# Argmax, gather and scatter: staging space first, spread list lanes, and row copies and zero scatters on semaphores of their own

## The chip, the cores and the metric

The kernel runs on one core of a Trainium2 chip. The metric is the time of the program on the device in microseconds. The span that the profile prints is about 2 us shorter than the time of the run.

## The reference

```python
def setup_inputs():
    B, S, H = (8, 2048, 2560)
    return {'scores': randn(B, S, S), 'values': randn(B, S, H)}     # float32

def reference(scores, values):
    best_j = np.argmax(scores, axis=2)
    b_idx = np.arange(B)[:, None]
    gathered = values[b_idx, best_j, :].copy()
    out = np.zeros_like(values)
    np.add.at(out, (b_idx, best_j, slice(None)), gathered)
    return out
```

Row j of a batch's output is its row of `values` times the number of score rows whose maximum lies at j. So the kernel counts the winners, and then each output row of 10,240 bytes is one of three things: count 0, a row of zeros; count 1, a copy of the row; count 2 or more, the row times the count.

## The kernel before

Counting: a tile of scores (256 rows, 2 MB, so 64 tiles in all and eight to a batch) comes in on the SP queue. DVE finds the maximum of each row and its place, and four small matmuls at a time add one-hot products into `cnt`. There are ten places for a tile: seven buffers of a pool, and three in `vbig`, the staging space that the values will use later. Before, loads 7, 8 and 9 go into `vbig`:

```python
    def count_steps(b, cnt_ps):
        for u in range(NT // R):                      # 8 tiles of a batch
            x = b * NT // R + u - NB                  # NB = 7, NX = 3
            if 0 <= x < NX:
                s_tile = vbig[:, x * R * S:(x + 1) * R * S]
            else:
                s_tile = spool.tile([P, R * S], FP32, name="s_tile")[:]
            nc.sync.dma_start(out=s_tile, in_=scores[...])
            ...                                       # max, max_index; a yield after each row
```

Values: when a batch is counted, its rows are sorted into lists. Rows of count 0 get a rank, and so do those of count 2 or more; rank r stands on lane (partition) r mod 128 in column r div 128. A transfer that POOL issues takes one column of 128 indices; an index outside of the bounds is skipped: its row doesn't move. Rows of count 1 need no rank: their 16 transfers copy straight from DRAM to DRAM.

```python
    def value_steps(b, cnt_ps):
        ...
        one_i = fin.tile([P, NT], INT32)              # a pool of two buffers
        ...
        for t in range(4):
            copy_once(t)
        ...                                           # ranks
        oh = ohp.tile([P, 2 * NT, P], FP16)
        nc.vector.tensor_tensor(out=oh[:], in0=lo[:]...,      # lo = rank & 127
            in1=lane_f[:].unsqueeze(1)..., op=ALU.is_equal)   # lane_f[lane] = lane
        ...
        for k in range(MCAP):                         # 5 columns of count >= 2
            v = stage()                               # one sixth of vbig
            gather(v, mi[:, k:k + 1])
            nc.scalar.activation(out=v, in_=v, ..., scale=mc[:, k:k + 1])
            staged.append(v)
            copy_once(next(rest))
        for k in range(ZCAP):                         # 7 columns of count 0
            scatter(zrow[:], zi[:, k:k + 1])
            copy_once(next(rest))
        for k in range(MCAP):
            scatter(staged[k], mi[:, k:k + 1])
        yield

        # ---- main loop
        for b in range(B):
            cnt_ps = psum_c.tile([P, NT], FP32)
            for _ in count_steps(b, cnt_ps):
                next(pending, None)                   # the values of b-1, between rows of b
            for _ in pending:
                pass
            pending = value_steps(b, cnt_ps)
```

The framework derives all waits from this program order: whoever comes later in it and touches the same memory waits for whoever comes earlier. Every transfer that POOL issues takes one of eight semaphores in turn, so POOL waits until the transfer issued eight before has landed.

## Time and profile before

| | before |
|---|---|
| time, median | 889.1 us |
| moved by the DMA engines | 347.05 MB, mean 391 GB/s |
| busy: DVE / POOL / ACT / PE | 687 / 290 / 103 / 18 us |
| DVE's longest single wait | 19.0 us, for `one_i` |

A DMA row of the slices is the mean of sixteen engines. A share of 0.95 can mean sixteen engines that are nearly always busy, or fifteen that wait for one.

### The profile page before, as it was taken

To read this page: it belongs to the slowest core of one execution; us is meant where nothing else is said; L and a number is where in the kernel's file an instruction comes from. 1 tells how busy PE (TensorE), PEld (TensorE's weight loads), DVE (VectorE), ACT (ScalarE), POOL (GpSimd) and SP (SyncE) were. 2 spreads that over 40 slices of the span, in tenths; PEclk is the share of its full clock that TensorE was granted. 3 is DMA by queue.
4 is the path that set the end of the run, shared out by engine and by line. 5 is a ranking of instruction groups with operands and counts; after the bars stand their busy time and mean duration, and the time that the engine had idled before them with its cause. 6 is when DMAs were issued, how large, how long until landed. Compare 5 with 4: busy or idle time off the path is not lost.

```text
span 888.3 us, 2271 instructions
## 1 busy us (share of the span) xinstructions
PE 18.0 (2%) x400; PEld 17.0 (2%) x400; DVE 687.3 (77%) x740; ACT 103.4 (12%) x43; POOL 290.3 (33%) x271
## 2 busy tenths in 40 slices
PE   0000000000000000000000000000000000000000
PEld 0000000000000000000000000000000000000000
DVE  6999999999999999999749994899919999000000
ACT  2000032000121000031001310023000500400500
POOL 0000452232323221521254222542234545544540
DMA  9998379999999999999999999999999998999994
GB/s 378 433 430 364 122 315 409 428 423 425 427 424 412 397 412 373 342 411 427 396 391 378 423 431 420 407 418 426 427 407 366 407 396 345 393 423 408 423 403 185
DMA packets 47248, 347.05 MB, mean 391 GB/s; under 512 B 18278, under 2 KB 18278, under 8 KB 18278
## 3 DMA queue, kind: packets, MB, share of 16 engines
q0 software_dynamic: 38016, 212.67, 59.2%
q1 hardware_dynamic: 9216, 134.22, 36.1%
q14 instruction: 13, 0.11, 0.0%
q8 instruction: 3, 0.05, 0.0%
HBM read 354.42 MB, written 293.60 MB: 729 GB/s over the span
## 4 chain that ended last, share of the span: by engine, by line
DMA 62%; DVE 28%; issue 4%; POOL 2%; POOLq 0%; DVEq 0%
DMA out_dram<-zrow,zero_i 31%; DMA vbig<-in_values_dram,many_i 12%; DVE am L147 12%; DMA out_dram<-vbig,many_i 12%; DVE mx L146 11%; DMA out_dram<-in_values_dram,one_i 6%; DVE oh L215 2%; POOL out_dram L33 1%; DMA s_tile<-in_scores_dram 1%; DVE oh_lo L156 1%; POOL vbig L113 1%; POOL out_dram L118 1%; DVE lo L152 0%; DVE rz L223 0%; DVE oh_hi L160 0%
## 5 line engine op out<-in xcount | busy, mean ns | idle before, releaser
L146 DVE MAX8 mx<-s_tile 128x8 f32<-128x2048 f32 x122 | 278.1, 2279 | 6.5 <-DMA s_tile<-in_scores_dram 6.5
L147 DVE FIND_INDEX8 am<-mx,s_tile 128x8 uint32<-128x2048 f32 x122 | 278.8, 2285 | 0.0
L33 POOL DMA_INDIRECT out_dram<-in_values_dram,one_i x128 | 129.2, 1009 | 249.3 <-DMA out_dram<-in_values_dram,one_i 103.3
L255 ACT ACTIVATE vbig<-vbig,many_c 128x2560 f32<-128x2560 f32 x40 | 97.1, 2428 | 737.6 <-DMA vbig<-in_values_dram,many_i 737.5
L118 POOL DMA_INDIRECT out_dram<-zrow,zero_i x56 | 57.9, 1034 | 159.4 <-DMA out_dram<-zrow,zero_i 77.4
L113 POOL DMA_INDIRECT vbig<-in_values_dram,many_i x40 | 60.0, 1501 | 82.2 <-DMA out_dram<-vbig,many_i 36.9
L118 POOL DMA_INDIRECT out_dram<-vbig,many_i x40 | 42.6, 1064 | 85.0 <-DMA out_dram<-zrow,zero_i 61.7
L179 DVE CAST one_i<-one_f 128x16 int32<-128x16 f32 x8 | 1.6, 196 | 52.8 <-DMA out_dram<-in_values_dram,one_i 52.2
L215 DVE TENSOR_TENSOR oh<-lo,lane_f 128x4096 f16<-128x4096 uint32 x8 | 35.4, 4426 | 0.0
L156 DVE TENSOR_TENSOR oh_lo<-lo,lane_f 128x512 bf16<-128x512 uint32 x32 | 22.2, 694 | 0.3
L165 PE MATMUL cnt_ps<-oh_hi,oh_lo 128*128 128x16 bf16 x128 | 8.1, 174 | 558.3 <-DVE oh_hi L160 558.3
L165 PEld LDWEIGHTS <-oh_lo 128*128 128x128 bf16 x128 | 8.4, 105 | 558.0 <-DVE oh_lo L156 556.9
L147 DVE MATCH_VALUE_LOAD am<-mx,s_tile 128x8 f32 x122 | 11.2, 92 | 4.2
L147 DVE FIND_INDEX8 am<-mx,vbig 128x8 uint32<-128x2048 f32 x6 | 13.7, 2285 | 0.0
L146 DVE MAX8 mx<-vbig 128x8 f32<-128x2048 f32 x6 | 13.7, 2281 | 0.0
L160 DVE TENSOR_TENSOR oh_hi<-hi,lane_f 128x64 bf16<-128x64 uint32 x32 | 7.0, 219 | 0.0
L234 PE MATMUL m_ps<-rm,oh 128*128 128x16 f16 x128 | 4.8, 175 | 86.0 <-DVE rm L230 86.0
L152 DVE TENSOR_SCALAR lo<-am 128x4 uint32<-128x4 uint32 x32 | 5.6, 176 | 1.1
L234 PEld LDWEIGHTS <-oh 128*128 128x128 f16 x128 | 4.1, 105 | 86.6 <-DVE rm L230 75.3
L154 DVE TENSOR_SCALAR hi<-am 128x4 uint32<-128x4 uint32 x32 | 5.6, 174 | 0.0
L237 PE MATMUL z_ps<-rz,oh 128*128 128x16 f16 x128 | 4.6, 174 | 0.0
L237 PEld LDWEIGHTS <-oh 128*128 128x128 f16 x128 | 4.0, 104 | 0.0
(50 smaller groups left out, 55.7 us busy)
## 6 DMA issues: line engine op xcount, KB each, us to landing
s_tile<-in_scores_dram SPq DMA_DIRECT2D x61, 2048.0 KB, 12.0
vbig<-in_scores_dram SPq DMA_DIRECT2D x3, 2048.0 KB, 38.9
out_dram<-in_values_dram,one_i POOLq DMA_INDIRECT x128
out_dram<-zrow,zero_i POOLq DMA_INDIRECT x56
vbig<-in_values_dram,many_i POOLq DMA_INDIRECT x40
out_dram<-vbig,many_i POOLq DMA_INDIRECT x40
```

What stands on the lines that cost most here:

```text
L33: return eng.add_instruction(ins)
L113: nc.gpsimd.indirect_dma_start(out=v, out_offset=None, in_=values_flat[:, :], in_offset=bass.IndirectOffsetOnAxis(ap=idx, axis=0), bounds_ ...
L118: writes_out(nc.gpsimd.indirect_dma_start(out=out_flat[:, :], out_offset=bass.IndirectOffsetOnAxis(ap=idx, axis=0), in_=v, in_offset=None, ...
L146: nc.vector.max(out=mx[:], in_=rows)
L147: nc.vector.max_index(out=am[:, g, :], in_max=mx[:], in_values=rows)
L156: nc.vector.tensor_tensor(out=oh_lo[:], in0=lo[:].unsqueeze(2).to_broadcast([P, G, P]), in1=lane_f[:].unsqueeze(1).to_broadcast([P, G, P]) ...
L160: nc.vector.tensor_tensor(out=oh_hi[:], in0=hi[:].unsqueeze(2).to_broadcast([P, G, NT]), in1=lane_f[:, 0:NT].unsqueeze(1).to_broadcast([P, ...
L165: nc.tensor.matmul(out=cnt_ps[:], lhsT=oh_lo[:, g, :], rhs=oh_hi[:, g, :], start=(t == 0), stop=(t == NT - 1))
L215: nc.vector.tensor_tensor(out=oh[:], in0=lo[:].unsqueeze(2).to_broadcast([P, 2 * NT, P]), in1=lane_f[:].unsqueeze(1).to_broadcast([P, 2 * ...
L234: nc.tensor.matmul(out=m_ps[:], lhsT=oh[:, NT + t, :], rhs=rm[:, t, :, :].rearrange("p a k -> p (a k)"), start=(t == 0), stop=(t == NT - 1))
L237: nc.tensor.matmul(out=z_ps[:], lhsT=oh[:, t, :], rhs=rz[:, t, :], start=(t == 0), stop=(t == NT - 1))
L255: nc.scalar.activation(out=v, in_=v, func=mybir.ActivationFunctionType.Copy, bias=0.0, scale=mc[:, k:k + 1])
```

## The change

Its intent, in three parts. First, scores use the staging space at once, for loads 0 to 2, and a second time for loads 10 to 12; batch 0's values are made in one block, before batch 1 is counted, with all 16 copies first, then zeros, then gathers. Second, the ranks of a column are spread over the lanes by a table `fill_f`, so that a column that is not full has work on all sixteen DMA engines. Third, copies and zero scatters get one semaphore per batch, outside the limit of 8 in flight, and POOL waits for all of them once at the end. The core of the diff (cuts marked):

```diff
+    for a in range(4):
+        first, step = (a >> 1) + 8 * (a & 1) + 16 * (a & 1), 16 - 32 * (a & 1)
+        nc.gpsimd.iota(fill_i[:, a * 32:(a + 1) * 32].rearrange("p (x y z) -> p x y z", x=4, y=2),
+                       pattern=[[2, 4], [step, 2], [32, 4]], base=first, channel_multiplier=0)
...
+    def free_running(b):
+        def note(ins):
+            writes_out(ins)
+            ins.then_inc(landed[b], 16)
+            tc.info.no_tile_sem_insts.add(ins.ins.name)
+            n_free[b] += 1
+        return note
...
-            x = b * NT // R + u - NB
-            if 0 <= x < NX:
+            x = b * NT // R + u
+            if x < 2 * (NX + NB) and x % (NX + NB) < NX:
+                x %= NX + NB
...
-        one_i = fin.tile([P, NT], INT32)
+        one_i = ones_i[:, b * NT:(b + 1) * NT]
...
-            writes_out(scatter_rows_in_dram(
+            free_running(b)(scatter_rows_in_dram(
...
-        for t in range(4):
+        first = NT if b == 0 else 4
+        for t in range(first):
             copy_once(t)
...
-            in1=lane_f[:].unsqueeze(1).to_broadcast([P, 2 * NT, P]), op=ALU.is_equal)
+            in1=fill_f[:].unsqueeze(1).to_broadcast([P, 2 * NT, P]), op=ALU.is_equal)
...
+        for part in (zeros, gathers) if b == 0 else (gathers, zeros):
+            part()
...
             pending = value_steps(b, cnt_ps)
+            if b == 0:
+                for _ in pending:
+                    pass
...
+    for b in range(B):
+        nc.gpsimd.wait_ge(landed[b], 16 * n_free[b])
```

More of the change, by code (lines that the diff above doesn't have):

```diff
@@ L75 @@
     nc.gpsimd.iota(lane_i[:], pattern=[[1, P]], base=0, channel_multiplier=0)
+    fill_i = consts.tile([P, P], INT32)
+    for a in range(4):
+        first, step = (a >> 1) + 8 * (a & 1) + 16 * (a & 1), 16 - 32 * (a & 1)
+        nc.gpsimd.iota(fill_i[:, a * 32:(a + 1) * 32].rearrange("p (x y z) -> p x y z", x=4, y=2),
+                       pattern=[[2, 4], [step, 2], [32, 4]], base=first, channel_multiplier=0)
     part_i = consts.tile([P, 1], INT32)
@@ L83 @@
     nc.vector.tensor_copy(lane_f[:], lane_i[:])
+    fill_f = consts.tile([P, P], FP32)
+    nc.vector.tensor_copy(fill_f[:], fill_i[:])
     part_f = consts.tile([P, 1], FP32)
@@ L95 @@
     nc.vector.memset(zero1[:], 0.0)
-    zrow = consts.tile([P, H], FP32)
+    zrow = ctx.enter_context(nc.sbuf_tensor([P, H], FP32))
     nc.scalar.copy(zrow[:], zero1[:].to_broadcast([P, H]))
@@ L101 @@
     nc.scalar.copy(vbig[:, NX * R * S:NV * H], zero1[:].to_broadcast([P, NV * H - NX * R * S]))
-    zero_i = lists.tile([P, B * NT], INT32)
+    ones_i = ctx.enter_context(nc.sbuf_tensor([P, B * NT], INT32))
+    zero_i = ctx.enter_context(nc.sbuf_tensor([P, B * NT], INT32))
     many_i = lists.tile([P, B * NM], INT32)
@@ L110, in writes_out @@
         tc.add_to_no_dep_group("out", ins.ins)
+    landed = [tc.alloc_semaphore(f"landed{b}") for b in range(B)]
+    n_free = [0] * B
+    def free_running(b):
[5 more added lines that the diff above has]
+        return note
     def gather(v, idx):
@@ L115, in gather, with scatter @@
             in_offset=bass.IndirectOffsetOnAxis(ap=idx, axis=0), bounds_check=B * S - 1, oob_is_err=False)
-    def scatter(v, idx):
-        writes_out(nc.gpsimd.indirect_dma_start(
+    def scatter(v, idx, note=writes_out):
+        note(nc.gpsimd.indirect_dma_start(
             out=out_flat[:, :], out_offset=bass.IndirectOffsetOnAxis(ap=idx, axis=0),
@@ L177, in value_steps @@
         nc.vector.scalar_tensor_tensor(out=one_f[:], in0=one_b[:], scalar=float(b * S), in1=row_f[:], op0=ALU.add, op1=ALU.add)
-        one_i = fin.tile([P, NT], INT32)
-        nc.vector.tensor_copy(one_i[:], one_f[:])
+        one_i = ones_i[:, b * NT:(b + 1) * NT]
+        nc.vector.tensor_copy(one_i, one_f[:])
         def copy_once(t):
-            writes_out(scatter_rows_in_dram(
+            free_running(b)(scatter_rows_in_dram(
                 nc, out_flat[:, :], values[b, t * P:(t + 1) * P, :], one_i[:, t:t + 1], last_row))
-        for t in range(4):
+        first = NT if b == 0 else 4
+        for t in range(first):
             copy_once(t)
@@ L248, in value_steps, with gathers, zeros @@
         nc.vector.tensor_copy(mc, m_ps[:, NM:2 * NM])
-        rest = iter(range(4, NT))
+        rest = list(range(first, NT))
         staged = []
-        for k in range(MCAP):
-            v = stage()
-            gather(v, mi[:, k:k + 1])
-            nc.scalar.activation(out=v, in_=v, func=mybir.ActivationFunctionType.Copy, bias=0.0, scale=mc[:, k:k + 1])
-            staged.append(v)
-            copy_once(next(rest))
-        for k in range(ZCAP):
-            scatter(zrow[:], zi[:, k:k + 1])
-            copy_once(next(rest))
+        def gathers():
+            for k in range(MCAP):
+                v = stage()
+                gather(v, mi[:, k:k + 1])
+                nc.scalar.activation(out=v, in_=v, func=mybir.ActivationFunctionType.Copy, bias=0.0,
+                                     scale=mc[:, k:k + 1])
+                staged.append(v)
+                if rest:
+                    copy_once(rest.pop(0))
+        def zeros():
+            for k in range(ZCAP):
+                scatter(zrow[:], zi[:, k:k + 1], free_running(b))
+                if rest:
+                    copy_once(rest.pop(0))
+        for part in (zeros, gathers) if b == 0 else (gathers, zeros):
+            part()
         for k in range(MCAP):
```

## The prediction

> **What bounds the kernel now.** I read the page's engine shares first, then its forty slices and queues, then windows laid around the places where the slices dip, and last the timeline of POOL.
>
> ```profile
> PE 18.0 (2%) x400; PEld 17.0 (2%) x400; DVE 687.3 (77%) x740; ACT 103.4 (12%) x43; POOL 290.3 (33%) x271
> ...
> DVE  6999999999999999999749994899919999000000
> ...
> DMA  9998379999999999999999999999999998999994
> GB/s 378 433 430 364 122 315 409 428 423 425 427 424 412 397 412 373 342 411 427 396 391 378 423 431 420 407 418 426 427 407 366 407 396 345 393 423 408 423 403 185
> ...
> q0 software_dynamic: 38016, 212.67, 59.2%
> q1 hardware_dynamic: 9216, 134.22, 36.1%
> ```
>
> No compute engine is the bound: DVE works 687 us of 888 and ends six slices before the kernel does. The DMA engines show 9 in all but five slices, and the two queues take 59.2 + 36.1 = 95.3% of their time. The third row has the two things to explain: a hole in slices 4 to 6, and a plateau that often falls below its own best of about 425 GB/s. The same span cut at those places (the last two columns are DMA share and GB/s):
>
> ```profile
> 66.00:78.00 12.00, 0.25 (x4) 0.26 (x4) 11.93 (x10) 0.00 (x0) 0.00 (x0) 1.00 1.01 433
> 78.00:122.00 44.00, 1.70 (x42) 1.66 (x42) 43.27 (x59) 0.88 (x1) 15.54 (x12) 1.00 0.50 183
> 122.00:182.00 60.00, 0.98 (x14) 0.91 (x14) 59.25 (x60) 11.26 (x5) 15.86 (x17) 1.00 1.01 421
> 182.00:700.00 518.00, 12.55 (x286) 11.76 (x286) 459.88 (x491) 53.41 (x22) 172.72 (x153) 1.00 0.99 407
> 700.00:760.00 60.00, 2.00 (x46) 1.85 (x46) 54.88 (x70) 7.62 (x4) 31.48 (x29) 1.00 0.95 376
> 760.00:860.00 100.00, 0.00 (x0) 0.00 (x0) 0.00 (x0) 23.93 (x10) 51.20 (x52) 1.00 1.01 411
> 860.00:876.00 16.00, 0.00 (x0) 0.00 (x0) 0.00 (x0) 0.00 (x0) 2.92 (x3) 1.00 0.93 386
> 876.00:888.00 12.00, 0.00 (x0) 0.00 (x0) 0.00 (x0) 0.00 (x0) 0.00 (x0) 1.00 0.10 42
> ```
>
> The packet records give the plateau by itself: the median 10,240-byte row on the software queue takes 385 ns, so one engine moves 26.6 GB/s and sixteen move 425.6. At that rate the 347.05 MB need 815 us. The last 12 us move almost nothing and the first 10 us lose about 3, so a kernel without any other loss would take 815 + 12 + 3 = 830 us. The 58 us above that are the prize, in two parts. The hole, 78 to 122 us, costs 44 x (1 - 183/425) = 25 us. The sagging plateau costs 518 x (1 - 407/425) = 22, plus 60 x (1 - 376/425) = 7, plus 100 x (1 - 411/425) = 3, plus 1: together 33 us.
>
> **Why the hole.** Tiles of scores hold two rows of work per partition and cost DVE about 9.7 us (two MAX8 of 2.28, two searches of 2.29, and half of the 1 us of counting); at the plateau they take the DMA 4.9 us. The loads therefore run ten tiles ahead until load 17, for which the pool has only seven buffers again, since the first use of the staging space as extra buffers (loads 7, 8, 9) is over. The values of batch 0 could fill the hole but start slowly:
>
> ```profile
> 91.93 1.12 POOL L33 DMA_INDIRECT out_dram<-in_values_dram,one_i  x1 [90.68 <-DVE m L190]
> ...
> 98.46 4.59 POOL L33 DMA_INDIRECT out_dram<-in_values_dram,one_i  x1 [0.30 <-issue]
> 114.53 1.03 POOL L113 DMA_INDIRECT vbig<-in_values_dram,many_i  x1 [11.48 <-DVE empty L246]
> ```
>
> The first copies go out at 92 us, then POOL waits 11.5 us for the lists, because the list work is spread over the next rows of scores on DVE.
>
> **Why the plateau sags.** Rows with count 0 and rows with count 2 or more are packed by rank into columns of 128 lanes, filled from lane 0 up. I counted the drawn inputs: a batch has 746 to 780 zero rows and 538 to 565 many rows, so the last many column has 26 to 53 rows, always in the lowest lanes, and five of the eight last zero columns hold 2 to 12.
>
> **What the Trainium skill says.**
> - "DMA: Bandwidth & Descriptors", section "The descriptor swizzle": in a 128-partition transfer each of the 16 engines serves eight partitions, engine = 8 x (partition >> 6) + ((partition >> 2) & 7). Low lanes are thus engines 0 to 7. The profile has no engine numbers, but the sag with a full queue agrees.
> - The same page, section "Queues, rings and completion order": each engine has its own ring and round-robins between queues. So a light engine cannot take rows of a heavy one. No view shows rings.
> - The same page, section "Where 436 GB/s comes from": a fabric ceiling of 435 GB/s. The trace agrees: 433 at best. I don't expect a faster plateau.
> - "SBUF — State Buffer", the box on "DVE blocks DMA": a DVE operation in a two-port mode locks GpSimd out of descriptor writing. The issue of 4.59 us above stands beside the 4.43 us `oh` comparison; the others take 0.98. That happens once per batch and stays.
>
> **The change, part by part.**
> 1. Spread lanes. With the swizzle and the counted rows, an engine moves 1,298 rows in the whole kernel on average. I assume that DRAM-to-DRAM copies split like partitions. Before, the two heaviest engines get 80 rows more than that; after, the heaviest gets 23 more. Check on before: 1,298 + 80 = 1,378 rows x 0.385 = 530 us, 512 score packets x 0.611 = 313 us, 10 us of semaphore packets: 853 us. With the hole (22 us by its share of 0.50) and 12 us of end it makes 887; measured 888. So the heaviest engine looks busy from start to end and **is** the bound. Gain: 57 x 0.385 = 22 us. The new fill table costs four small iotas and one DVE copy at the start, hidden beside the first load.
> 2. Staging space first. Now loads 0 to 2 and 10 to 12 use it, so loads run ten ahead until load 19, not 16. Batch 0's values come at once: its list work is no longer interleaved (some 10 us of DVE in a block), all its 16 copies go out at 1.3 us each from about 91, and its zeros follow. Copies are 7.7 MB and zeros 7.8 MB, together 36 us of DMA, so from 91 to about 140 it is full with loads 17 to 19 beside it. Gathers must wait for tiles 10 to 12, read at about 131 to 151 us. Load 20 needs tile 13, about 161. I expect smaller dips, some 13 us before 91 at half share and some between 145 and 185: in all 8 to 14 us in place of 25. A lower limit: by the end of batch 1's counting, about 182 us, at most 23 tiles (48 MB) and batch 0's values (26.5 MB) can have moved, 75 MB against 77 at the plateau. So the hole can nearly close, but this is my least certain term. Gain: 14 us.
> 3. Own semaphores. Copies and zero scatters no longer wait for the transfer eight before. POOL's waits on DMA (139 and 103 us are the largest) mostly vanish, and so do DVE's 52.2 us before `one_i`, since each batch has its own. None of it is on the path while the queues are full. What it buys is that engines may drift apart, so random unevenness of the copies no longer holds up the rest. I book 2 us. The eight waits at the end are on work that must land anyway.
>
> Sum: 889 - 22 - 14 - 2 = 851. From below: 830 + 23 x 0.385 (9) + a hole of 11 = 850. I put 3 us on it for slow packets (the mean row takes 398 ns, not 385): **853 us**.
>
> **The rivals.**
> - A: the bytes bind alone and unevenness is hidden (the mean share is 0.95 already). For: windows at share 1.01 with only 411 GB/s, so packets get slower rather than engines idle. Then part 1 gives 5 us at most: 865 to 872.
> - B: the hole only moves. Gathers of batch 0 now wait for tile 12, and DVE is stopped 10 us earlier for lists. For: DVE makes a tile in 9.7 us whatever happens, and the seven-deep pool returns at load 20. Against: the 75 MB above. Then part 2 gives 0 to 5: 860 to 867.
> - C: deep queues of copies delay the scores on the same engines, and DVE becomes the bound. DVE needs 687 us plus the values of the last batch, some 65 us: 760 plus the end. Too far from 850 to bind.
> - D: both gains full and the hole closed: 838.
>
> **Range and chances.** D gives the low end, 838; A or B with a little loss beside it gives the high end, 872. The line of 2% is 871, which needs A and B together. Faster 0.87, same 0.11, slower 0.02.
>
> **What will show it.** MB moved stay 347. Part 1: 182 to 700 us should rise from 407 to at least 418 GB/s. Part 2: slices 4 to 6 over 350 GB/s; look for a new dip at 145 to 185. Part 3: `one_i` waits gone, POOL waits on its own DMA small, DVE done before 715 us, and the last six slices full. If the rate stays at 407, my lane count is wrong; if a dip as large as the old stands later, the hole was supply from DVE.

## The result and the profile after

The changed kernel takes 908.98 us (908.92 to 909.32, 4 runs) against 889.12: the ratio is 1.0222, 95% interval 1.0204 to 1.0239. Here and below a ratio is the mean time of one kernel's fast runs over that of the other's of the same rounds, so not quite the ratio of the medians. The change makes the kernel 20 us slower, where I had forecast 36 us faster.

The page of the changed kernel, with the same rows as the first view of the prediction (busy us; DVE's, the DMA's and the GB/s slices; the two queues):

```profile
PE 18.0 (2%) x400; PEld 16.9 (2%) x400; DVE 687.8 (76%) x741; ACT 102.9 (11%) x43; POOL 275.7 (30%) x275
...
DVE  6999820499999999999999999999999994000000
...
DMA  9920899999779999999999999999999999999991
GB/s 381 428 116 12 260 401 424 373 428 381 286 304 417 426 426 429 427 426 424 429 427 424 429 427 426 427 427 426 428 429 418 423 425 423 423 424 421 424 399 53
...
q0 software_dynamic: 38016, 212.67, 57.0%
q1 hardware_dynamic: 9216, 134.22, 35.1%
```

The bytes are the same, and DVE has as much work. Two things changed in opposite directions. From slice 13 to 38 the plateau is flat at 417 to 429 GB/s where it used to sag to 342. But the start is worse: slice 4 moves 12 GB/s, and slices 8 and 10 to 12 dip again, down to 286. DVE, which used to work through this stretch, falls to 2 and 0 in slices 6 and 7. Cut at these places (share of the DMA and GB/s are the last columns):

```profile
50.00:90.00 40.00, 0.70 (x10) 0.65 (x10) 39.10 (x47) 0.00 (x0) 1.92 (x2) 1.00 0.05 18
90.00:122.00 32.00, 1.26 (x36) 1.27 (x36) 25.18 (x27) 0.00 (x0) 25.29 (x23) 1.00 0.85 285
122.00:160.00 38.00, 0.00 (x0) 0.00 (x0) 0.00 (x0) 12.03 (x5) 9.74 (x10) 1.00 1.01 424
160.00:182.00 22.00, 0.00 (x0) 0.00 (x0) 11.52 (x9) 0.00 (x0) 0.00 (x0) 1.00 0.91 373
...
220.00:260.00 40.00, 1.74 (x42) 1.58 (x42) 39.31 (x56) 0.00 (x0) 11.96 (x9) 1.00 0.69 252
260.00:700.00 440.00, 11.27 (x250) 10.54 (x250) 434.56 (x460) 48.45 (x20) 134.63 (x131) 1.00 1.01 426
...
880.00:900.00 20.00, 0.00 (x0) 0.00 (x0) 0.00 (x0) 0.00 (x0) 0.00 (x0) 1.00 0.32 132
```

The same bookkeeping as in the prediction, time lost against 425 GB/s:

| | before | after |
|---|---|---|
| bytes at 425.6 GB/s | 815 | 815 |
| first load | 3 | 2 |
| holes near the start | 25 | 38 + 11 + 3 + 16 = 68 |
| sagging plateau | 33 | 1 |
| end | 12 | 14 + 7 = 21 |
| sum | 888 | 907 |

So the plateau gave back 32 us, and the end took 9 of them: that is the row of 0.32 above, where about five of sixteen engines' time was used. The start took 43.

What stopped the start stands in the timeline of the SP queue of the changed kernel (start, length, loads):

```profile
0.75 1.33 SPq L160 DMA_DIRECT2D vbig<-in_scores_dram  x3
2.12 11.50 SPq L160 DMA_DIRECT2D s_tile<-in_scores_dram  x7
159.17 12.00 SPq L160 DMA_DIRECT2D vbig<-in_scores_dram  x3
171.28 502.50 SPq L160 DMA_DIRECT2D s_tile<-in_scores_dram  x51
```

After the tenth load none is issued for 145 us. The kernel before issued its eleventh at 18 us:

```profile
0.75 3.56 SPq L138 DMA_DIRECT2D s_tile<-in_scores_dram  x7
4.34 9.25 SPq L138 DMA_DIRECT2D vbig<-in_scores_dram  x3
18.19 134.77 SPq L138 DMA_DIRECT2D s_tile<-in_scores_dram  x11
```

And the waits of the changed kernel, of the SP queue first, then of DVE (total, times, longest), name what ended them:

```profile
SPq L160 <- DMA out_dram<-vbig,many_i: 156.2, 3, 145.4
...
DVE mx L168 <- DMA vbig<-in_scores_dram: 58.0, 2, 52.1
```

In the kernel before, DVE's one wait for scores is short:

```profile
DVE mx L146 <- DMA s_tile<-in_scores_dram: 6.5, 1, 6.5
```

Load 10 waited 145.4 us for a scatter **out of** the staging space, a piece of batch 0's values; DVE then waited 52.1 us for load 10. In program order batch 0's values stand before batch 1's counting, since the new loop drains them there. Their gathers write `vbig` and their scatters read it; load 10, the third of batch 1, overwrites it, so it has to wait until they are done. Loads 11 and 12 have the same kind of wait. SP issues in order, so loads 13 and later stand behind them, though their buffers were long free. DVE had its ten tiles and ran dry at 118 us. The dip from 220 to 260 us is another matter. No load waits for a scatter there, DVE is busy for 39.31 of the 40 us, and batch 1's first copies go out only at 234 us: a hole of the old kind, with loads seven ahead at DVE's pace and no values to move yet.

The theory to test: **the order of gathers and load 10 makes the whole loss; spread lanes pay what was forecast; the own semaphores pay nothing.** The rival: the loss comes from the flood of 23 unlimited transfers of batch 0, or from its block of list work, and the load is only where it shows.

### The profile page after: what moved, and what is told of

It is laid out like the page before. It is cut to its first block, busy times and chain, and to the rows that moved or that the text cites. A ratio compares the mean times of both kernels' runs of the same rounds, so it can differ in the third digit from the quotient of the medians.

```text
span 907.4 us, 2251 instructions
## 1 busy us (share of the span) xinstructions
PE 18.0 (2%) x400; PEld 16.9 (2%) x400; DVE 687.8 (76%) x741; ACT 102.9 (11%) x43; POOL 275.7 (30%) x275
## 4 chain that ended last, share of the span: by engine, by line
DVE 68%; DMA 11%; POOL 9%; issue 7%; POOLq 0%; PE 0%; SPq 0%; DVEq 0%
DVE am L169 30%; DVE mx L168 28%; DMA out_dram<-vbig,many_i 9%; POOL out_dram L33 5%; POOL out_dram L139 3%; DVE oh L239 3%; DMA vbig<-in_scores_dram 2%; DVE oh_lo L178 2%; POOL vbig L134 1%; DVE lo L174 1%; DVE oh_hi L182 0%; DVE rz L247 0%; DVE hi L176 0%; DVE ez L243 0%; DVE rank L233 0%
## 5 line engine op out<-in xcount | busy, mean ns | idle before, releaser
L169 DVE FIND_INDEX8 am<-mx,s_tile 128x8 uint32<-128x2048 f32 x116 | 265.0, 2285 | 0.0
L168 DVE MAX8 mx<-s_tile 128x8 f32<-128x2048 f32 x116 | 264.3, 2278 | 0.0
L33 POOL DMA_INDIRECT out_dram<-in_values_dram,ones_i x128 | 134.7, 1052 | 228.6 <-DVE m L214 190.4
L134 POOL DMA_INDIRECT vbig<-in_values_dram,many_i x40 | 42.1, 1052 | 228.3 <-DMA out_dram<-vbig,many_i 193.0
L139 POOL DMA_INDIRECT out_dram<-vbig,many_i x40 | 39.0, 976 | 110.6 <-ACT vbig L280 104.6
L168 DVE MAX8 mx<-vbig 128x8 f32<-128x2048 f32 x12 | 27.4, 2280 | 58.0 <-DMA vbig<-in_scores_dram 58.0
L239 DVE TENSOR_TENSOR oh<-lo,fill_f 128x4096 f16<-128x4096 uint32 x8 | 35.4, 4428 | 0.0
L169 DVE FIND_INDEX8 am<-mx,vbig 128x8 uint32<-128x2048 f32 x12 | 27.4, 2285 | 0.0
L247 DVE TENSOR_TENSOR rz<-ez,row_f 128x256 f16<-128x256 f16 x8 | 3.4, 429 | 0.3
```

Of the source, the lines that this page charges most:

```text
L33: return eng.add_instruction(ins)
L134: nc.gpsimd.indirect_dma_start(out=v, out_offset=None, in_=values_flat[:, :], in_offset=bass.IndirectOffsetOnAxis(ap=idx, axis=0), bounds_ ...
L139: note(nc.gpsimd.indirect_dma_start(out=out_flat[:, :], out_offset=bass.IndirectOffsetOnAxis(ap=idx, axis=0), in_=v, in_offset=None, bound ...
L168: nc.vector.max(out=mx[:], in_=rows)
L169: nc.vector.max_index(out=am[:, g, :], in_max=mx[:], in_values=rows)
L239: nc.vector.tensor_tensor(out=oh[:], in0=lo[:].unsqueeze(2).to_broadcast([P, 2 * NT, P]), in1=fill_f[:].unsqueeze(1).to_broadcast([P, 2 * ...
```

## The experiments

Each kernel was timed in three rounds beside the kernel before, on the same chip, and each gave a correct result. The experiments ran on three chips; the kernel before took 888.62, 888.38 and 888.77 us on them, so times of different chips are compared as they are. The parts of the change are first put alone on the kernel before.

**The new staging and order alone.** The edit on the kernel before is the staging, the order of batch 0 and the early drain of the diff above, without `fill_f` and with `writes_out` in place of `free_running`:

```diff
-            x = b * NT // R + u - NB
-            if 0 <= x < NX:
+            x = b * NT // R + u
+            if x < 2 * (NX + NB) and x % (NX + NB) < NX:
+                x %= NX + NB
...
+            if b == 0:
+                for _ in pending:
+                    pass
```

> The kernel before with the new use of the staging space and the new order of batch 0 alone. Theory (load 10 goes into staging space that the gathers and scatters of batch 0 use first in program order, so it and all later loads wait for those scatters): slower than before by 30 to 45 us, 920 to 935, with no score load between about 52 and 155 us and DVE idle for some 50 us on a staging load. Rival (it is the flood of free-running transfers): within 10 us of before.

Measured: 931.19 us, ratio 1.0477 (1.0460 to 1.0495), 42.6 us slower. Loads stop until 159.75 us again, and the wait is there with the limit of 8 in force:

```profile
159.75 12.74 SPq L139 DMA_DIRECT2D vbig<-in_scores_dram  x3
...
DVE mx L147 <- DMA vbig<-in_scores_dram: 62.0, 2, 55.2
```

The flood is not needed for the loss.

**Spread lanes alone.**

```diff
-            in1=lane_f[:].unsqueeze(1).to_broadcast([P, 2 * NT, P]), op=ALU.is_equal)
+            in1=fill_f[:].unsqueeze(1).to_broadcast([P, 2 * NT, P]), op=ALU.is_equal)
```

> The kernel before with the spread list lanes alone. Theory (the heaviest DMA engine binds the plateau): about 867 us, 22 below before, and from 182 to 700 us the rate rises from 407 to 418 GB/s or more. Rival (unevenness is hidden behind the mean share): 884 to 889, rate as before. The hole of 78 to 122 us stays at about 25 us in both.

Measured: 869.05 us, ratio 0.9775 (0.9758 to 0.9791), so 19.6 us faster. The hole is as before and the plateau rose from 407 to 421 GB/s:

```profile
78.00:122.00 44.00, 1.70 (x42) 1.66 (x42) 43.27 (x59) 1.04 (x1) 15.48 (x12) 1.00 0.49 181
182.00:700.00 518.00, 12.77 (x290) 11.98 (x290) 476.49 (x505) 60.59 (x25) 179.85 (x163) 1.00 1.01 421
```

**Own semaphores alone** (the parts `free_running`, `ones_i` and the waits at the end; with them go `zrow` and `zero_i`, which move out of their pools into plain SBUF tensors).

```diff
-            writes_out(scatter_rows_in_dram(
+            free_running(b)(scatter_rows_in_dram(
...
-            scatter(zrow[:], zi[:, k:k + 1])
+            scatter(zrow[:], zi[:, k:k + 1], free_running(b))
```

> The kernel before with the own semaphores (and an index tile per batch) alone. Theory: 884 to 889, because the heaviest engine has as many rows as before; DVE's waits at the index cast vanish. Rival (the unlimited queue is what makes the changed kernel slower, since score loads come late behind it): 895 or more, with DVE waiting for scores. Rival 2 (the limit of 8 made the plateau sag): 870 or less.

Measured: 888.65 us, ratio 0.9997 (0.9981 to 1.0014). The waits of DVE for `one_i`, 52 us, are gone, POOL's copies and zero scatters no longer wait for the transfer eight before, and the time is the same. This run shows best what binds. Its windows:

```profile
182.00:700.00 518.00, 13.52 (x300) 12.65 (x300) 511.16 (x547) 56.18 (x24) 168.89 (x159) 1.00 1.00 417
700.00:850.00 150.00, 1.02 (x32) 0.93 (x32) 3.74 (x14) 28.79 (x12) 71.23 (x71) 1.00 0.99 406
850.00:860.00 10.00, 0.00 (x0) 0.00 (x0) 0.00 (x0) 0.00 (x0) 0.00 (x0) 1.00 0.76 320
860.00:876.00 16.00, 0.00 (x0) 0.00 (x0) 0.00 (x0) 0.00 (x0) 0.00 (x0) 1.00 0.19 78
```

The plateau went from 407 to 417, since light engines may now run ahead, but they only finish early: from 860 to 876 us a share of 0.19 is the work of about three engines, and the end comes when it did. In a recount of the drawn inputs with the prediction's formula, three engines have 61 to 81 rows more than the mean and the next one 35. The uneven work was moved from the plateau into the tail.

**Spread lanes and own semaphores together, staging and order of before.**

> Spread lanes and own semaphores on the kernel before, staging space and order of before. Theory: 858 to 867, the hole of before kept (25 us), the plateau at 425 GB/s as in the changed kernel: over 40 us faster than the changed kernel. If the two parts need each other, this is clearly under the sum of the two single gains. Rival (free-running transfers cost something): 875 or more.

Measured: 870.50 us, ratio 0.9786 (0.9770 to 0.9802). That misses the range by 3 us. The plateau is flat, 425 GB/s from 182 to 700 us, but the end pays for it: 760 to 860 us move 358 GB/s, against 395 with spread lanes alone. Beside the 869.05 of spread lanes alone, the semaphores add nothing to them either.

**The changed kernel with the lanes packed again** (the one line of `fill_f` undone).

> The changed kernel with the lanes filled from 0 up again. Theory (the heaviest engine has 57 rows of 0.385 us more): 22 us above the changed kernel, 929 to 933, the plateau unchanged at about 425 GB/s but a long tail in which few engines are busy. Rival (with a queue without limit the unevenness averages out): within 8 of the changed kernel, up to 917.

Measured: 933.13 us, ratio to the kernel before 1.0498 (1.0480 to 1.0515), 24.2 us above the changed kernel. The long tail came, a share of 0.15 from 900 to 930 us; the unchanged plateau didn't, single slices fall to 345 GB/s. The unevenness costs about the same in either schedule (19.6 and 24.2 us), as it should if it is a sum over the whole kernel.

**Another fill table, to see which lanes share an engine.** No view names an engine. So on the kernel before, ranks were laid engine by engine as the formula of the Trainium skill has it ("DMA: Bandwidth & Descriptors", section "The descriptor swizzle"), a bad order if the formula holds for these transfers:

```diff
+    nc.gpsimd.iota(fill_i[:].rearrange("p (h a e z) -> p h a e z", h=2, a=2, e=8),
+                   pattern=[[64, 2], [4, 2], [8, 8], [1, 4]], base=0, channel_multiplier=0)
...
+            in1=fill_f[:].unsqueeze(1).to_broadcast([P, 2 * NT, P]), op=ALU.is_equal)
```

> The kernel before with one other fill table: the lanes are filled so that the first eight ranks of a column sit on lanes 0 to 3 and 32 to 35, the next eight on 4 to 7 and 36 to 39, and so on, the lanes that share an engine by the skill's formula. Theory (that formula, heaviest engine binds): the heaviest engine goes from 81 rows above the mean to 125, so 17 us slower than before, 903 to 908. Rival (eight neighbouring lanes share an engine): its heaviest goes from 125 to 120, so within 3 us of before.

Measured: 910.18 us, ratio 1.0241 (1.0220 to 1.0262), 21.4 us slower. That is 2 us outside of the range and some 4 more than 44 rows of 0.385 us make; where these 4 come from stays open. The plateau sags further, from 407 to 398 GB/s:

```profile
182.00:700.00 518.00, 12.54 (x286) 11.74 (x286) 448.06 (x483) 48.56 (x20) 166.47 (x146) 1.00 0.98 398
```

The rival, eight neighbouring lanes to an engine, is ruled out. Three tables on one kernel, 869, 889 and 910 us, follow the heaviest engine's 23, 81 and 125 rows above the mean. The packed traces also show how the unevenness hides behind a share of 0.98 to 1.01: the median row packet takes 385 ns in all three, but the mean 394, 398 and 403 ns, so a part of the lost time stands in a few long packets and not as idle engines. Which engines have them no view shows. How the copies from DRAM to DRAM are split was not tried; the counts assume the same formula for them.

**The changed kernel with its gathers after load 12.** This is the schedule that I had in mind when I predicted. Ten steps of batch 1's counting are put between batch 0's zeros and gathers:

```diff
-        for part in (zeros, gathers) if b == 0 else (gathers, zeros):
-            part()
+        if b == 0:
+            zeros()
+            for _ in range(10):
+                yield
+            gathers()
+        else:
+            gathers()
+            zeros()
...
             if b == 0:
-                for _ in pending:
-                    pass
+                for _ in range(4):
+                    next(pending)
```

> The changed kernel with one move: batch 0's gathers stand after load 12 and its reading in program order, so the gathers wait for the loads and not the loads for the scatters. This is the schedule that the prediction had in mind. Theory (the order alone made the loss): 850 to 860, loads go on past 52 us, no DVE wait on a staging load above 10 us, and a smaller dip between 145 and 185 us. Rival (the flood of 23 free transfers of batch 0, or the block of list work, holds up the loads): over 880.

Measured: 860.07 us, ratio 0.9677 (0.9661 to 0.9693): 49 us faster than the changed kernel from the order of one group of five gathers, with the flood of copies and the block of list work still there. The staging loads go out at 18 us, DVE's wait for them falls from 58.0 to 6.1 us, and POOL waits for DVE's reading instead (the last column), each time a few us:

```profile
18.43 19.24 SPq L160 DMA_DIRECT2D vbig<-in_scores_dram  x3
...
127.92 1.04 POOL L134 DMA_INDIRECT vbig<-in_values_dram,many_i  x1 [6.22 <-DVE am L169]
132.51 0.99 POOL L134 DMA_INDIRECT vbig<-in_values_dram,many_i  x1 [3.55 <-DVE am L169]
...
DVE mx L168 <- DMA vbig<-in_scores_dram: 6.1, 1, 6.1
```

That settles the rival. The dip that I looked for at 145 to 185 us came later, from 190 to 210, and it moved 237 GB/s.

**The changed kernel without a second use of the staging space.** Two ways: loads 0 to 2 only (`if x < NX:`), or loads 5 to 7, the last of batch 0 (`x = b * NT // R + u - (NT // R - NX)`, `if 0 <= x < NX:`).

> The changed kernel with the staging space used for loads 0 to 2 only and never again for scores. Theory: no load waits for a scatter, but loads run seven ahead from load 10, so the DMA falls to half rate from about 52 to 88 us (18 us lost) and dips a little later: 860 to 868. Rival (early list work and the flood of batch 0 hurt by themselves): over 885.

> The changed kernel with the staging space used for loads 5 to 7, the last of batch 0, and never again for scores. Theory: ten ahead until load 14, then load 15 waits for tile 8 at about 108 us; a hole of some 15 us from 73 to 88 us in place of the 43 us hole: 855 to 865, better than the use for loads 0 to 2 by 3 to 8. Rival as there: over 885.

Measured: 866.34 us (ratio 0.9751, 0.9731 to 0.9771) and 865.83 us (0.9743, 0.9720 to 0.9767). Both drop the wait on the scatters, and both are over 40 us faster than the changed kernel, so the theory holds a second time by another way. The difference of 3 to 8 us between them didn't come, probably because seven-deep loading is back in both by the time batch 0's values start, and it makes no difference whether the DMA is slowed from 55 us on or runs in full and then stops at 77: from 50 to 90 us they move 10 and 11 MB.

**The limit of 8 back in the good schedule.** The run with gathers after load 12, with `writes_out` in place of `free_running` and no waits at the end.

> The run with batch 0's gathers after load 12, but copies and zero scatters back under the limit of 8 in flight. Theory (own semaphores are worth about nothing): within 5 us of 860. Rival (they pay once the lanes are spread and the hole is closed): 868 or more.

Measured: 860.03 us, ratio 0.9681 (0.9665 to 0.9697), against 860.07 with own semaphores. In four pairs (the last point of this document has them) they were worth nothing that can be told from noise.

**A version that beats both.** From the run with gathers after load 12, two edits for the two dips left: batch 0's zeros alternate with its last eight copies (in the changed kernel, copies alone moved 344 GB/s from 100 to 110 us at a share of 0.98), and every batch's list work is done in one block at the end of its counting.

```diff
-        first = NT if b == 0 else 4
+        first = 8 if b == 0 else 4
...
                 for _ in range(4):
                     next(pending)
+            else:
+                for _ in pending:
+                    pass
```

> The changed kernel with batch 0's gathers after load 12, its zeros interleaved with its last eight copies, and the list work of every batch in one block at the end of its counting. Theory: fills the two dips that were left (80 to 120 us with copies alone in the queue, 190 to 210 us while batch 1's lists were interleaved): 848 to 856. Rival (what is left is the supply of DVE, which a reordering does not raise): 858 to 862.

Measured: 849.95 us, ratio to the kernel before 0.9563 (0.9547 to 0.9579). Its slices have one deep dip left, at 292:

```profile
GB/s 377 428 428 426 292 416 420 420 405 421 425 427 427 427 428 428 428 423 428 425 426 425 429 427 428 424 429 424 428 425 422 424 426 417 425 425 420 426 374 41
```

The stretch from 182 to 210 us moves 404 GB/s. How the 10 us divide between the two edits was not tried. The windows point to the list work: 80 to 122 us went only from 338 to 353 GB/s, which is 1.5 us, while the dip to 237 is gone.

## Why the prediction was wrong

- **Part 2, the staging space, is the step that failed.** The prediction put it so: "Gathers must wait for tiles 10 to 12, read at about 131 to 151 us." The wait runs the other way: tiles 10 to 12 wait for the gathers' scatters. I had read which loads share memory with which gathers, but not which of them comes first in the program. The three lines that drain batch 0's values before batch 1's counting make that plain, but they are not needed for it: with the old interleaving, by the code, the gathers would be made at batch 1's fourth step, and load 10 comes with its fifth. Only a move like that of the 860 us run puts them behind load 12. The lower limit of 75 MB asked how many bytes could move, not which load was free to. A gain of 14 us was booked, and the part alone measured a loss of 42.6.
- The size of that loss follows from the right order (the holes of 68 in place of 25 us in the table). Ten loads are all there is, so the DMA is empty from about 51 us until the copies at 88; DVE has ten tiles and stops at 118; load 10 is issued at 159 and read from 170.
- **Part 1, spread lanes, was right** in mechanism and nearly in size: 22 us forecast, 19.6 on the kernel before and 24.2 within the change. The plateau rose as named (at least 418 was asked for): 182 to 700 us went from 407 to 421 with the lanes alone. In the changed kernel the same window has 413, since the dip at 220 to 260 us lies in it; from 260 us on it is 426. The 9 us that I had left for the heaviest engine agree with the end, 21 in place of 12 us. But that the check on before came to 887 was in part luck: it took median packet times, 385 and 611 ns, and with the mean times of the same packets, 398 and 626, it makes 913. The three fill tables show the bound, not that sum. Two readings beside it were off: of the "10 us of semaphore packets" some 7 are those of skipped rows (13,030 of 17,254), and 433 GB/s is not before's best, since one window of 10 us moves 436.
- **Part 3, own semaphores, was booked at 2 us and is worth 0.** What they should buy, engines that drift apart, does happen. It helps nobody while one engine's sum is the bound. POOL's waits on DMA didn't become small either: 193 us remain before gathers, for scatters out of the staging space. DVE, forecast to be done before 715 us, worked on until 750 to 760.
- **Rival B** ("the hole only moves") named DVE's supply and gathers that wait for tile 12. It came nearest in kind, and it also assumed the wrong direction; its 860 to 867 is what the schedule of the prediction would have given, as the 860 us run shows. My 853 for that schedule was 7 us too low: the dips were larger, about 18 us by the same bookkeeping, than the 11 that I left for them. Rivals A and C fell: the bytes' unevenness does show, and scores that come late behind a deep queue were seen in no run. No rival had a load wait for a scatter, and slower was given a chance of 0.02.

## What to carry to other kernels

When a buffer gets a second use, write down both users in program order before asking who waits for whom: the order of issue decides the direction of the wait, and a queue that issues in order lets one such wait stop every load behind it. With an indirect transfer, a column of indices that isn't full can put its rows on few DMA engines, and these remainders add up over the kernel (869, 889 and 910 us here for three tables): spread the filled lanes over the engines. A limit on transfers in flight, or a wait of 52 us on an engine that is not the bound, may cost nothing; ask which engine's sum ends the kernel.

## What the Trainium skill lacked or had wrong

- "DMA: Bandwidth & Descriptors", section "The descriptor swizzle": it gives the formula for a plain 128-partition transfer. The runs agree with it for indirect gathers and scatters with skipped indices (869, 889 and 910 us for three fill tables), and the page doesn't say what becomes of skipped rows: each leaves a packet of 4 bytes and 9 ns in place of 385 ns, so the filled lanes decide the load. 58 rows less on the heaviest engine's sum were worth 19.6 us.
- The same page, section "Latency and other measured facts": its figure for copies between HBM tensors is 214 GB/s per direction at full rate, on other queues and with 16 KiB rows. With copies of single rows alone in the queue the changed kernel moved 344 GB/s from 100 to 110 us, so 214 is no ceiling for such copies; it is still below the 426 of the mixed plateau, and no page says so.
- No page says what a limit on transfers in flight costs. Here lifting it, for copies and zero scatters, was worth 0 us within the noise (with the limit and without: 889 and 889, 869 and 871, 931 and 933, 860 and 860).
